# Layer 1 of a two-layer mixer and PEER kernel: the second table's products in two rounded parts

## The chip, the cores and the metric

The kernel runs on 1 core of a Trainium2 chip. The time is the device time of one execution in microseconds (us). The engines are called TensorE (PE; its weight loads are shown apart as PEld), VectorE (DVE), ScalarE (ACT), GpSimd (POOL) and SyncE (SP, which issues most transfers). The trace is of one profiled execution.

## What is computed

A backbone of two layers works on 256 latent tokens and 256 context tokens of width 1024. Each layer has a token mixer and then a feed-forward network of 16384 single-neuron experts (PEER). Only the latter matters here. For every token it chooses 16 experts for each of 8 heads, by two short lists of keys, and adds up the chosen rows of a second table, `v_tab`, each weighted by a softmax and by the gelu of the token's product with the row of a first table, `u_tab`:

```python
def peer_ffn(x, w_q, keys, u_tab, v_tab):
    def chunk(t):
        q = (t @ w_q).astype(jnp.float32).reshape(PEER_CHUNK, PEER_HEADS, 2, PEER_DK // 2)
        s = jnp.einsum("thpc,hpnc->thpn", q, kf)
        sv, si = lax.top_k(s, PEER_TOPK)
        ...
        best, pos = lax.top_k(cand, PEER_TOPK)
        eidx = jnp.take_along_axis(cidx, pos, axis=-1)
        g = jax.nn.softmax(best, axis=-1)
        act = jax.nn.gelu(jnp.einsum("thkd,td->thk", jnp.take(u_tab, eidx, axis=0), t).astype(jnp.float32))
        w = (g * act).astype(t.dtype)
        return jnp.einsum("thk,thkd->td", w, jnp.take(v_tab, eidx, axis=0))
```

The output is the latent stream after the second layer and a final norm.

## The kernel before

The program is a list of items for each layer: the mixer's, then the network's (`peer`). `Builder.run` goes through the list, and each item issues its instructions on all engines in the order of the code; nothing reorders them later, so the order of the items sets the order on every engine.

The network is computed densely for most tokens. Stage *up* (`up`, 128 items): for each block of 128 experts the first table's block times the tokens, with gelu, into the large buffer `A` (experts x blocks x tokens). Beside it DVE chooses the experts (`topk`, `weights`). Stage *experts* (`experts`, one item for four tokens): from the lists, one-hot matrices `oi` and `oj` are made, their product `psG` holds each token's softmax weights at its experts, and `A` is multiplied by it (L1366). Stage *down* (`down`, 126 items and one of two blocks): for each block of 128 experts, eight products of a 128x128 block of the second table with a row of `A`, summed over all blocks in four banks of PSUM called `acc`. `end` adds the sum to the stream and, in layer 1, applies the final norm. In layer 1 only 160 latent tokens go this way (N = 160; in layer 0 it is 256). The rest of the tokens, in layer 1 96, go the sparse way: their experts' rows are fetched one by one by GpSimd's indirect transfers (L1219) and added up by PE in `psC` with weights `wl` (`far_up`, `far_down`). Its steps are issued between the items by `far_go`, 18 of them in layer 1's *down*. What they fetch goes into the buffers `own` and `hs`, which the change leaves as they are. The last step copies `psC` into `ct` on ACT and turns it by eight transposes.

A product on PE comes in two forms. Unrounded: one matmul of 32-bit operands (L1502, layer 1's *down*; L1321, *up*). Rounded: both operands are given as a high part, rounded to the type fp32r, and a low part, the rest, rounded as well; `mm3` adds three matmuls of them, high by high, high by low and low by high (L200, L201, L202). The low by low product is left out. The mixers and layer 0's *down* use it. The parts are made by `cut` (for a half of a table's row block, 512 columns: a copy on ACT, L174, and a subtraction on DVE or GpSimd, L176 or L178; `lo_by` says on which, in *down* always DVE) and by `halves` (for `A`: L205, L206, called by `w_halves` for two blocks at once). `run` makes the cuts up to CUT = 5 halves ahead of the item that needs them.

The raw rows of the tables come by SP's transfers, 512 KB each. In layer 1 they go through a ring of eight buffers, five lent from the cuts' pool (`fetched`) and three of the pool `raw`; a ring piece is not cut, and its buffer is free again when its item is done. `self.lent` says that the cuts' own pool is lent away. Layer 1's network further has buffers of its own: `xe`, `h` (normed input), `qT` (queries), `rt` (routing: the lists' scratch), `keys`, `hs`, `own`, `wh` and `cand`. `h`, `qT`, `rt` and `keys` are last read before or during the *experts* stage's start; `wh` holds `oj` in that stage and then `ct`.

Of the kernel before, what the change touches and what calls it, by code (L numbers as in the profile page):

```python
# [69 lines left out]
class Builder:  # L70
# [21 lines left out]
    def run(self, items):  # L92
# [4 lines left out]
        cuts = [(p, h) for p in loads for h in range(p.cuts())]  # L97
        self.raws = self.rings = n_cut = used = n_ring = 0

        def load():  # L100
            nonlocal n_ring
            while rings and rings[0].ring == self.ring_for and self.rings < len(self.ring):
                p = rings.pop(0)
                p.raw = self.ring[n_ring % len(self.ring)]
                n_ring += 1
                self.rings += 1
                self.nc.sync.dma_start(out=p.raw[:, :p.width], in_=p.ap)
            while loads and self.raws < self.RAW and n_ring >= 16:
                p = loads.pop(0)
                p.at = n  # L110
                p.raw = self.wp.tile([128, 1024], F, tag="raw", name="raw", bufs=self.RAW)
                self.raws += 1
                self.nc.sync.dma_start(out=p.raw[:, :p.width], in_=p.ap)

        n = 0
        for n, it in enumerate(items):
            if n:
                load()
            now = used + sum(p.cuts() for p in it.pieces)
            while cuts and not self.lent and n_cut < used + self.CUT and cuts[0][0].raw is not None:  # L120
                if n_cut >= now and (n < max(cuts[0][0].at + self.AGE, self.FIRST) or not it.ahead):
                    break
                self.cut(*cuts.pop(0))
                n_cut += 1
                load()
            self.new = []
            it.fn(*it.pieces)
            used += sum(p.cuts() for p in it.pieces)
            self.raws -= sum(p.keep and p.ring is None for p in it.pieces)
            self.rings -= sum(p.ring is not None for p in it.pieces)  # L130
            self.tick()
# [27 lines left out]
    turn, lo_by, ring_for = 0, "vp", None  # L159
    lent = False  # L160
# [6 lines left out]
    def cut(self, p, h):  # L167
        nc = self.nc
        a, b = h * 512, min(h * 512 + 512, p.width)
        both = self.wp.tile([128, 2, 512], R, tag="cut", name="whl", bufs=self.CUT)  # L170
# [9 lines left out]
        if b == p.width and not p.keep:  # L180
            self.raws -= 1
# [825 lines left out]
    def peer(self, l, seg, far):  # L1007
# [27 lines left out]
        def begin():  # L1035
# [15 lines left out]
            else:  # L1051
                xs, h32, qT = (mp.tile([128, 8, 256], F, name=n) for n in ("xe", "h", "qT"))
                rt, keys = (mp.tile([128, 1024], F, name=n) for n in ("rt", "keys"))
# [302 lines left out]
        def experts(t4):  # L1356

            def fn():
# [15 lines left out]
                if t4 == N // 4 - 1:  # L1374
                    self.flush()
                    self.lo_by = self.LO_DOWN
            return Item(fn)


        def far_down():  # L1380
# [16 lines left out]
            for s, (tt, m) in enumerate(steps):  # L1397
# [22 lines left out]
                if m == nf - 1:  # L1420
                    while two and hold["i"] < 28:
                        yield False
                    ct = flat(A[:, 16:20]) if two else mp.tile([128, 2, 1024], F, tag="wh", name="ct")[:, 0]
# [51 lines left out]
        def down(i, n=1):  # L1475

            def fn(*ps):
                nonlocal wh
                hold["i"] = i
                if i == 0:  # L1480
# [3 lines left out]
                    if two:  # L1484
                        wh = mp.tile([128, 2, 4, 256], R, tag="wh", name="wh")
                        w_halves(0)
                if two:
                    if i % 2 == 0 and i < 126:
                        w_halves(i + 2)
# [6 lines left out]
                for d in range(8):  # L1496
                    for j, p in enumerate(ps):
                        acc, first, last = hold["acc"][d // 2][:, d % 2, :N], i == 0 and d % 2 == 0, i + j == 127
                        if two:
                            self.mm3(acc, p.block(d), wt[i + j], first, last, skip=True)  # L1500
                        else:
                            nc.tensor.matmul(acc, p.raw[:, d * 128:d * 128 + 128], A[:, i + j], start=first, stop=last,  # L1502
                                             skip_group_check=True)
# [5 lines left out]
            return Item(fn, *[Piece(t["peer_v"][l, j * 128:j * 128 + 128], 1024, split=two, ring=ring) for j in range(i, i + n)],  # L1509
# [160 lines left out]
```

## Time and profile before

| | us |
|---|---|
| median of 3 runs | 3388.54 (3386.39 to 3388.63) |
| profiled execution | 3395.13 |
| its span, first to last instruction | 3393.4 |
| in the span: layer 1's *experts* stage | 2984 to 3062 |
| layer 1's *down* | 3062 to 3379 |
| `end`, last part | 3379 to 3393 |

The profile is a page with the busy time of each engine, slices of the span and groups of instructions, and views of the trace that answer narrower questions. PE and PEld count instructions as the hardware records them: an unrounded matmul leaves two records, a rounded one leaves one, and each record has a weight load beside it. A matmul's duration reaches from its start to the modelled end of its pipeline, so records overlap, and the pace is read from start to start. "PEclk" is the granted clock of PE as a share of 2.4 GHz.

### The profile page before, as it was taken

The numbers are of one execution on the slowest core, as the hardware profiler recorded it, in microseconds if no ns is written. First come the engines' busy times: TensorE is split into PE (matmuls) and PEld (weight loads), VectorE is DVE, ScalarE is ACT, GpSimd is POOL, SyncE is SP. The second block draws the span as 40 slices with busy tenths as digits, with TensorE's granted clock in tenths as the row PEclk, the third lists the DMA queues.
The fourth block names the chain that finished last, engine by engine and source line by source line (L and its number), as shares of the span: only waits on it lengthen the run. The fifth ranks groups of instructions, "written<-read, shape, count | busy, mean of one in ns | idle before, by whom it ended". The sixth has DMA issues, their size and how long they took to land. (4 is left out here: it accounts for less than half of the span.)

```text
span 3393.4 us, 50776 instructions
## 1 busy us (share of the span) xinstructions
PE 3111.5 (92%) x19130; PEld 2514.0 (74%) x19130; DVE 1893.5 (56%) x4591; ACT 1076.3 (32%) x2268; POOL 1250.6 (37%) x1178
## 2 busy tenths in 40 slices
PE   7999999997799999588999998988998999989998
PEld 4667776785688788346777787667878899868897
DVE  6557444444799997866444455566444767660001
ACT  4554344331101101254333344554554110160000
POOL 2422223320254445674445512334453044372220
PEclk9999999998999999699999998999999999989999
DMA  7421221234699999976999966542235699968995
GB/s 273 156 98 57 68 60 60 87 118 149 228 400 387 375 378 407 333 255 229 343 373 393 392 242 214 168 134 87 95 100 172 213 387 408 402 209 312 353 354 184
DMA packets 245013, 819.03 MB, mean 241 GB/s; under 512 B 31776, under 2 KB 50464, under 8 KB 244512
## 3 DMA queue, kind: packets, MB, share of 16 engines
q1 hardware_dynamic: 137824, 441.40, 36.9%
q0 software_dynamic: 101376, 369.14, 29.1%
q10 hardware_dynamic: 5568, 5.24, 0.5%
q8 instruction: 151, 2.47, 0.3%
q14 instruction: 94, 0.77, 0.1%
HBM read 809.37 MB, written 6.29 MB: 240 GB/s over the span
## 5 line engine op out<-in xcount | busy, mean ns | idle before, releaser
L178 POOL TENSOR_TENSOR whl<-raw,whl 128x512 fp32r<-128x512 f32 x249 | 326.3, 1325 | 820.0 <-ACT whl L174 735.2
L176 DVE TENSOR_TENSOR whl<-raw,whl 128x512 fp32r<-128x512 f32 x359 | 277.6, 781 | 387.2 <-ACT whl L174 316.4
L1321 PE MATMUL psA<-hb,raw 128*128 128x256 f32 x2048 | 458.9, 383 | 14.6 <-DMA raw<-peer_u 12.7
L174 ACT ACTIVATE whl<-raw 128x512 fp32r<-128x512 f32 x608 | 362.0, 626 | 318.6 <-PE acc L202 249.3
L1321 PEld LDWEIGHTS psA<-hb,raw 128*128 128x128 f32 x2048 | 385.6, 191 | 80.9 <-issue 11.0
L200 PE MATMUL psA<-hhi,whl 128*128 128x512 f32 (+1 forms) x1032 | 375.6, 364 | 10.5 <-DVE bones L459 6.6
L201 PE MATMUL psA<-hlo,whl 128*128 128x512 f32 (+1 forms) x1032 | 365.3, 354 | 0.3 <-POOL hlo L506 0.3
L202 PE MATMUL psA<-hhi,whl 128*128 128x512 f32 (+1 forms) x1032 | 364.0, 353 | 0.9 <-DVE whl L176 0.9
L1219 POOL DMA_INDIRECT fetched<-u_rows,ft x184 | 184.0, 1000 | 322.9 <-PE psN L1214 136.6
L200 PE MATMUL acc<-wh,whl 128*128 128x256 f32 x1024 | 294.8, 288 | 1.4 <-ACT wh L205 1.4
L201 PE MATMUL acc<-wh,whl 128*128 128x256 f32 x1024 | 289.6, 283 | 0.8 <-issue 0.4
L202 PE MATMUL acc<-wh,whl 128*128 128x256 f32 x1024 | 289.4, 283 | 0.0
L1323 ACT ACTIVATE A<-psA 128x512 f32<-128x512 f32 (+1 forms) x128 | 66.2, 517 | 691.4 <-PE psA L1321 591.9
L200 PEld LDWEIGHTS psA<-hhi,whl 128*128 128x128 f32 x1032 | 198.7, 193 | 61.5 <-issue 26.5
L1250 DVE SCALAR_TENSOR_TENSOR fetched<-fetched,hT 128x1024 f32<-128x1024 f32 x184 | 221.3, 1209 | 22.1 <-DMA fetched<-u_rows,ft 15.5
L200 PEld LDWEIGHTS acc<-wh,whl 128*128 128x128 f32 x1024 | 195.9, 191 | 40.3 <-issue 23.5
L202 PEld LDWEIGHTS psA<-hhi,whl 128*128 128x128 f32 x1032 | 198.2, 192 | 28.0 <-DVE whl L176 1.9
L201 PEld LDWEIGHTS psA<-hlo,whl 128*128 128x128 f32 x1032 | 197.9, 192 | 25.0 <-POOL hlo L506 0.6
L201 PEld LDWEIGHTS acc<-wh,whl 128*128 128x128 f32 x1024 | 196.1, 192 | 0.5 <-DVE wh L206 0.5
L202 PEld LDWEIGHTS acc<-wh,whl 128*128 128x128 f32 x1024 | 196.1, 192 | 0.5 <-issue 0.5
L1219 POOL DMA_INDIRECT hb<-peer_v,ft x136 | 141.3, 1039 | 146.6 <-PE psC L1413 113.7
L1219 POOL DMA_INDIRECT own<-u_rows,ft x96 | 104.0, 1083 | 243.4 <-DVE own L1250 99.8
(372 smaller groups left out, 6043.9 us busy)
## 6 DMA issues: line engine op xcount, KB each, us to landing
raw<-peer_u SPq DMA_DIRECT2D x176, 512.0 KB
raw<-peer_v SPq DMA_DIRECT2D x176, 512.0 KB
raw<-w_in SPq DMA_DIRECT2D x126, 512.0 KB
ring<-w_mod SPq DMA_DIRECT2D x88, 512.0 KB
fetched<-peer_u SPq DMA_DIRECT2D x80, 512.0 KB
fetched<-peer_v SPq DMA_DIRECT2D x80, 512.0 KB
raw<-w_branch SPq DMA_DIRECT2D x32, 512.0 KB
raw<-w_out SPq DMA_DIRECT2D x16, 512.0 KB
```

The lines of the kernel that those rows point to most:

```text
L174: nc.scalar.activation(hx, x, AF.Copy)
L176: nc.vector.tensor_sub(lx, x, hx.bitcast(F))
L178: nc.gpsimd.tensor_sub(lx, x, hx.bitcast(F))
L200: mm(ps, wh, xh, start=start, stop=False, skip_group_check=skip)
L201: mm(ps, wh, xl, start=False, stop=False, skip_group_check=skip)
L202: mm(ps, wl, xh, start=False, stop=stop, skip_group_check=skip)
L1219: nc.gpsimd.indirect_dma_start(out=buf, out_offset=None, in_=rows, in_offset=bass.IndirectOffsetOnAxis(ap=idx.bitcast(I32), axis=0))
L1250: nc.vector.scalar_tensor_tensor(b, b, 1.0, h, op0=OP.mult, op1=OP.mult, accum_out=f[:, 3, k:k + 1])
L1321: nc.tensor.matmul(ps[:, :N], p.raw[:, k * 128:k * 128 + 128], h32[:, k, off:], start=k == 0, stop=k == 7)
L1323: nc.scalar.activation(A[:, i - 1:i + 1, :], hold["ps"][:, :, :N], AF.Gelu_apprx_tanh)
```

## The change

In layer 1's *down* the products are made as in layer 0, by `mm3` from two rounded parts. The ring's pieces of the second table are now split: `run` lists their cuts too (`pieces` in place of `loads`), notes when they were loaded, and gives a ring buffer back when its piece has been cut. `cut` takes its output from `cut_to`, where that is set, in place of the pool `cut`, which in layer 1 is lent to the ring. `cut_to` is set in the last `experts` item: six buffers of 128 x 2 x 512, two each in the place of `h`, `qT` and `rt`, for which `rt` and `keys` become two halves of one buffer; `lent` becomes false there, so that the cutting can begin with the first `down` item. The row of `A` is split by `w_halves` into `wh`, and `ct` moves from `wh` to `cand`.

```diff
@@ -94,13 +94,14 @@
         pieces = [p for it in items for p in it.pieces]
         loads = [p for p in pieces if p.ring is None]
         rings = [p for p in pieces if p.ring is not None]
-        cuts = [(p, h) for p in loads for h in range(p.cuts())]
+        cuts = [(p, h) for p in pieces for h in range(p.cuts())]
         self.raws = self.rings = n_cut = used = n_ring = 0
 
         def load():
             nonlocal n_ring
             while rings and rings[0].ring == self.ring_for and self.rings < len(self.ring):
                 p = rings.pop(0)
+                p.at = n
                 p.raw = self.ring[n_ring % len(self.ring)]
                 n_ring += 1
                 self.rings += 1
@@ -127,7 +128,7 @@
             it.fn(*it.pieces)
             used += sum(p.cuts() for p in it.pieces)
             self.raws -= sum(p.keep and p.ring is None for p in it.pieces)
-            self.rings -= sum(p.ring is not None for p in it.pieces)
+            self.rings -= sum(p.keep and p.ring is not None for p in it.pieces)
             self.tick()
 
 
@@ -157,6 +158,7 @@
             self.new = []
 
     turn, lo_by, ring_for = 0, "vp", None
+    cut_to = None
     lent = False
 
     def lo(self, l, i):
@@ -167,7 +169,10 @@
     def cut(self, p, h):
         nc = self.nc
         a, b = h * 512, min(h * 512 + 512, p.width)
-        both = self.wp.tile([128, 2, 512], R, tag="cut", name="whl", bufs=self.CUT)
+        if self.cut_to:
+            both = self.cut_to[self.turn % len(self.cut_to)]
+        else:
+            both = self.wp.tile([128, 2, 512], R, tag="cut", name="whl", bufs=self.CUT)
         hi, lo = both[:, 0], both[:, 1]
         p.parts.append((hi, lo))
         x, hx, lx = p.raw[:, a:b], hi[:, :b - a], lo[:, :b - a]
@@ -178,7 +183,10 @@
             nc.gpsimd.tensor_sub(lx, x, hx.bitcast(F))
         self.turn += 1
         if b == p.width and not p.keep:
-            self.raws -= 1
+            if p.ring is None:
+                self.raws -= 1
+            else:
+                self.rings -= 1
 
 
     def open(self, name, banks=True):
@@ -1049,8 +1057,9 @@
                 h32 = hb[:, 0]
                 own = [flat(hb[:, a, r:r + 4]) for a in range(2) for r in (0, 4)]
             else:
-                xs, h32, qT = (mp.tile([128, 8, 256], F, name=n) for n in ("xe", "h", "qT"))
-                rt, keys = (mp.tile([128, 1024], F, name=n) for n in ("rt", "keys"))
+                xs, h32, qT = (mp.tile([128, 8, 256], F, tag=n, name=n) for n in ("xe", "h", "qT"))
+                both = mp.tile([128, 2, 1024], F, tag="rt", name="rt")
+                rt, keys = both[:, 0], both[:, 1]
                 fq, fh = qT, h32
                 hs = mp.tile([128, 2, 1024], F, name="hs")
                 own = [mp.tile([128, 1024], F, name=f"own{i}") for i in range(6)]
@@ -1371,9 +1380,13 @@
                     if "far" not in hold:
                         hold["far"], hold["done"] = far_steps(), 0
                     far_go(EARLY + 1 if last else min(hold["done"] + 1, (EARLY + 1) * (t4 + 1) // (N // 4 - 4)))
-                if t4 == N // 4 - 1:
+                if last:
                     self.flush()
                     self.lo_by = self.LO_DOWN
+                    if not two:
+                        w = [mp.tile([128, 2, 2, 512], R, tag=tag, name="whl") for tag in ("h", "qT", "rt")]
+                        self.cut_to = [x[:, i] for x in w for i in range(2)]
+                        self.lent = False
             return Item(fn)
 
 
@@ -1420,7 +1433,7 @@
                 if m == nf - 1:
                     while two and hold["i"] < 28:
                         yield False
-                    ct = flat(A[:, 16:20]) if two else mp.tile([128, 2, 1024], F, tag="wh", name="ct")[:, 0]
+                    ct = flat(A[:, 16:20]) if two else mp.tile([128, 1024], F, tag="cand", name="ct", bufs=1)
                     for h in range(2):
                         nc.scalar.activation(ct[:, h * 512:h * 512 + 512], c[h], AF.Copy)
                     yield True
@@ -1481,12 +1494,11 @@
                     hold.pop("oj")
                     hold.pop("oi")
                     hold["acc"] = [psT([128, 2, 256], "acc") for _ in range(4)]
-                    if two:
-                        wh = mp.tile([128, 2, 4, 256], R, tag="wh", name="wh")
-                        w_halves(0)
+                    wh = mp.tile([128, 2, 4, N], R, tag="wh", name="wh")
+                    w_halves(0)
+                if i % 2 == 0 and i < 126:
+                    w_halves(i + 2)
                 if two:
-                    if i % 2 == 0 and i < 126:
-                        w_halves(i + 2)
                     if i == 28:
                         hold["xf"] = A[:, 20:28]
                         nc.sync.dma_start(out=hold["xf"], in_=self.xs[far])
@@ -1496,17 +1508,13 @@
                 for d in range(8):
                     for j, p in enumerate(ps):
                         acc, first, last = hold["acc"][d // 2][:, d % 2, :N], i == 0 and d % 2 == 0, i + j == 127
-                        if two:
-                            self.mm3(acc, p.block(d), wt[i + j], first, last, skip=True)
-                        else:
-                            nc.tensor.matmul(acc, p.raw[:, d * 128:d * 128 + 128], A[:, i + j], start=first, stop=last,
-                                             skip_group_check=True)
+                        self.mm3(acc, p.block(d), wt[i + j], first, last, skip=True)
                 for j in range(n):
                     wt.pop(i + j, None)
                 slow = 4 if two else 0
                 far_go(EARLY + (i + 1) // 4 if i < 4 * slow else
                        EARLY + slow + (FAR - EARLY - slow) * (i + 1 - 4 * slow) // (122 - 4 * slow))
-            return Item(fn, *[Piece(t["peer_v"][l, j * 128:j * 128 + 128], 1024, split=two, ring=ring) for j in range(i, i + n)],
+            return Item(fn, *[Piece(t["peer_v"][l, j * 128:j * 128 + 128], 1024, ring=ring) for j in range(i, i + n)],
                         ahead=i + n < 128)
 
         def end():
```

PE at the start of layer 1's *down* (`psC` is the sparse way's sum, `psG` the one-hot product, `acc` the dense sum). Before:

```order
L1413 MATMUL psC<-own_20866,wl 32x512
L1413 MATMUL psC<-hs,wl 32x512 x2
L1364 MATMUL psG<-oi,oj 128x128 x16
L1502 MATMUL acc<-A,fetched 128x160 x40
L1502 MATMUL acc<-A,raw 128x160 x24
L1502 MATMUL acc<-A,fetched 128x160 x32
```

And now:

```order
L1426 MATMUL psC<-own_20865,wl 32x512
L1426 MATMUL psC<-hs,wl 32x512 x2
L1373 MATMUL psG<-oi,oj 128x128 x16
L208 MATMUL acc<-wh,whl 128x160
L209 MATMUL acc<-wh,whl 128x160
L210 MATMUL acc<-wh,whl 128x160
```

Each product of 160 columns has become three, on the rounded parts `wh` and `whl`; what stands ahead and the places of `psC` between the blocks are as before.

DVE at the same place (`oi` and `oj` are the one-hot matrices, `wl` the sparse way's weights, `whl` a cut half, `wh` the split row of `A`). Before:

```order
L1366 TENSOR_TENSOR A<-A,psG 128x128x4
L1351 TENSOR_SCALAR oi<-iota,sel 128x128
L1352 TENSOR_TENSOR oj<-iota,sel 128x512
L1366 TENSOR_TENSOR A<-A,psG 128x128x4 x4
L1401 TENSOR_TENSOR wl<-ft,zero_20881 128x128 x18
L1432 SCALAR_TENSOR_TENSOR xe<-psX,mod_86,xe 128x96 x8
```

And now:

```order
L1375 TENSOR_TENSOR A<-A,psG 128x128x4
L1360 TENSOR_SCALAR oi<-iota,sel 128x128
L1361 TENSOR_TENSOR oj<-iota,sel 128x512
L1375 TENSOR_TENSOR A<-A,psG 128x128x4 x4
L181 TENSOR_TENSOR whl<-fetched,whl 128x512 x5
L214 TENSOR_TENSOR wh<-A,wh 128x320 x2
L181 TENSOR_TENSOR whl<-fetched,whl 128x512 x4
L214 TENSOR_TENSOR wh<-A,wh 128x320
```

Behind the last multiplications into `A`, where the 18 `wl` stood alone, five subtractions of cut halves now come first, then the first two pairs of `A`'s parts, and so on through the stage with the `wl` between them.

## Rows read from the trace of the kernel before

**Rows 1.** The page: span, busy us, share and instructions of the engines.

```profile
span 3393.4 us, 50776 instructions
PE 3111.5 (92%) x19130; PEld 2514.0 (74%) x19130; DVE 1893.5 (56%) x4591; ACT 1076.3 (32%) x2268; POOL 1250.6 (37%) x1178
```

**Rows 2.** Busy time by stretch: busy us and instructions, granted clock, DMA share, GB/s.

```profile
core 0: us, PE busy (x) PEld busy (x) DVE busy (x) ACT busy (x) POOL busy (x), PEclk, DMA share, GB/s
3062.00:3379.00 317.00, 316.26 (x2344) 287.07 (x2344) 10.48 (x38) 3.44 (x8) 64.27 (x67) 1.00 0.86 312
```

**Rows 3.** The chain that ended last: start us, us, engine, tile, line, instructions.

```profile
3062.23 26.35 PE acc L1502 x192
3088.58 1.85 PE psC L1413 x16
3090.43 13.24 PE acc L1502 x96
```

**Rows 4.** Groups from 3062 to 3379 us: busy us, mean ns, idle before, releaser.

```profile
L1502 PE MATMUL acc<-A,fetched 128*128 128x160 f32 x1280 | 179.5, 300 | 0.8 <-DVE A L1366 0.8
L1502 PE MATMUL acc<-A,raw 128*128 128x160 f32 x768 | 108.2, 300 | 0.0
L1413 PE MATMUL psC<-own,wl 128*32 128x512 f32 x216 | 34.5, 598 | 0.0
L1413 PE MATMUL psC<-hs,wl 128*32 128x512 f32 x72 | 17.2, 598 | 0.0
```

**Rows 5.** Instructions in order of time, PE, within layer 1's down.

```profile
3092.64 6.68 PE L1502 MATMUL acc<-A,raw 128*128 128x160 f32 x48
```

**Rows 6.** The same, PE in layer 0's down: rounded products, 256 columns.

```profile
2002.14 0.28 PE L200 MATMUL acc<-wh,whl 128*128 128x256 f32 x1
2002.26 0.28 PE L201 MATMUL acc<-wh,whl 128*128 128x256 f32 x1
```

**Rows 7.** The same, PE in layer 0's mixer: rounded products, 512 columns.

```profile
689.89 0.39 PE L200 MATMUL psA<-ohi,whl 128*128 128x512 f32 x1
...
692.15 0.39 PE L201 MATMUL psA<-hlo,whl 128*128 128x512 f32 x1
```

**Rows 8.** The same, weight loads in layer 0's down after a pause.

```profile
1614.51 0.19 PEld L200 LDWEIGHTS acc<-wh,whl 128*128 128x128 f32 x1 [0.84 <-ACT wh L205]
1614.61 0.19 PEld L201 LDWEIGHTS acc<-wh,whl 128*128 128x128 f32 x1
1614.73 0.19 PEld L202 LDWEIGHTS acc<-wh,whl 128*128 128x128 f32 x1
```

**Rows 9.** The same, weight loads of unrounded products with 96 columns.

```profile
429.80 1.86 PEld L212 LDWEIGHTS psT<-ones,sq 128*128 128x128 f32 x16 [1.61 <-ACT sq L816]
```

**Rows 10.** Groups from 1574 to 2048 us, layer 0's down.

```profile
L200 PEld LDWEIGHTS acc<-wh,whl 128*128 128x128 f32 x940 | 179.8, 191 | 38.6 <-issue 23.5 <-ACT wh L205 14.2 <-ACT whl L174 0.8
L176 DVE TENSOR_TENSOR whl<-raw,whl 128x512 fp32r<-128x512 f32 x233 | 160.0, 692 | 252.2 <-ACT whl L174 188.8 <-issue 60.0
L174 ACT ACTIVATE whl<-raw 128x512 fp32r<-128x512 f32 x234 | 146.2, 630 | 283.5 <-PE acc L202 243.4 <-DMA raw<-peer_v 19.0 <-issue 14.9
L206 DVE TENSOR_TENSOR wh<-A,wh 128x512 fp32r<-128x512 f32 x59 | 40.4, 685 | 0.0
```

**Rows 11.** Instructions in order of time where layer 1's down begins.

```profile
3061.49 0.69 DVE L1366 TENSOR_TENSOR A<-A,psG 128x512 f32<-128x512 f32 x1 [0.21 <-issue]
...
3062.23 11.13 PE L1502 MATMUL acc<-A,fetched 128*128 128x160 f32 x80 [0.78 <-DVE A L1366]
```

**Rows 12.** The same, PE where layer 0's down begins.

```profile
1573.20 0.38 PE L200 MATMUL acc<-wh,whl 128*128 128x256 f32 x1 [1.44 <-ACT wh L205]
...
1573.93 0.38 PE L201 MATMUL acc<-wh,whl 128*128 128x256 f32 x1 [0.34 <-DVE wh L206]
```

**Rows 13.** Busy time by stretch, columns as in rows 2.

```profile
2750.00:2800.00 50.00, 50.00 (x370) 49.42 (x369) 39.90 (x112) 4.81 (x11) 21.89 (x21) 1.00 1.02 408
```

**Rows 14.** Transfers from 3062 to 3379 us.

```profile
DMA packets 27129, 99.01 MB, mean 312 GB/s; under 512 B 3020, under 2 KB 3020, under 8 KB 27107
```

## The prediction

> **What bounds the kernel now.** I read the page first, for the shares of the engines [rows 1]: TensorE (PE) is busy for 92% of the span and, apart from its own weight loads, no other engine for more than 56%. That is a mean over very different stages, so the next view is the busy time by stretch [rows 2]. The change touches one stretch, the second table's products of layer 1, from 3062 us to 3379 us. There PE is busy for 316.26 of 317.00 us at a granted clock of 1.00, which is the upper of its two levels, 2.4 GHz. VectorE (DVE) works for 10.48 us of it, ScalarE (ACT) for 3.44 us, and the DMA moves 312 GB/s. The chain of waits says the same in another way [rows 3]: from 3062.23 us its links are two kinds of PE work in turn, 13.24 us for 96 records of the products `acc` and 1.85 us for the 16 records of `psC`, and so on to the stage's end. Nothing ends late there but PE, so this stage is worth exactly what its matmuls cost, and a change of their number or pace goes into the span in full. The groups of that stretch give the counts [rows 4]: 1280 + 768 = 2048 records of `acc` for 128 blocks of experts x 8 = 1024 products, two records for each unrounded product.
>
> **What the change removes.** It removes the 1024 unrounded products. In a stretch without interruption 48 records take 6.68 us, each 0.299 us long [rows 4, 5], so one starts every (6.68 - 0.30) / 47 = 0.1358 us, and 2048 of them cost 278.1 us. The rest of the stage stays: (216 + 72) / 16 = 18 steps of `psC` at 1.85 us, 33.3 us, and some 5 us of changes between the two kinds.
>
> **What it adds on PE.** Each product becomes three rounded ones of one record each (layer 0's rows show L200, L201 and L202 taking turns), so 3072 records, and each has its own load of 128 columns of weights. What one such record costs with 160 columns is the whole question, and the trace has no rounded product with fewer than 256 columns. It can be bounded from both sides:
>
> - With 256 columns a rounded record starts every 0.120 us [rows 6]; with 512 columns every 0.226 us: ten steps in 2.26 us from 689.89 to 692.15 [rows 7]. The slope is 0.107 us for 256 columns, with about 0.013 us on top. Carried on to 160 columns, that gives 0.067 + 0.013 = 0.080 us, if columns alone set the pace.
> - The weights must be loaded as well. In layer 0's rounded stream, just after a pause, when two loads may follow each other freely, they still start 0.10 us apart, and from then on 0.12 us [rows 8]. And where a product has so few columns that its streaming cannot hide the load, the load sets the pace: 16 unrounded records with 96 columns (2 x 96 = 192 columns streamed, which by the slope above would be done in 0.080 us) have loads that take 1.86 us from first start to last end, at 0.19 us each, so one every (1.86 - 0.19) / 15 = 0.111 us [rows 9].
>
> So I take max(0.080, 0.111), rounded to 0.112 us: a product with 160 rounded columns waits for its weights. It is the row nearest in kind, a stream whose columns take less than its load. 3072 x 0.112 = 344.1 us, which is 66.0 us more than the 278.1 us that go. The ends: at the 0.105 us that the closest pair of loads allows, 322.6 us, +44.5; at 0.120 us, the pace that layer 0's rounded stream really holds, 368.6 us, +90.5.
>
> The Trainium skill states a price for the load in "TensorE: Matmul & The Clock Gate", section "LDWEIGHTS (loading the stationary operand)": columns divided by 1.2 GHz, so 107 ns for 128. That rule speaks against this change, and the trace agrees with it (0.111 us by the 96-column stream). By it alone the sum would be 3072 x 0.107 = 328.7 us, an estimate, +50.6 us.
>
> **What it adds on ACT and DVE.** For each block two halves of the raw table are rounded (ACT) and subtracted (DVE), and for every second block a pair of the weights' columns. From layer 0's same stage: 0.630 us and 0.692 us a half, and on DVE 0.685 us a pair with 512 elements [rows 10]; layer 1's pair has 320, so that is an upper bound, and I take it for ACT too. For each block of 128 experts, ACT: 2 x 0.63 + 0.34 = 1.60 us. DVE: 2 x 0.69 + 0.34 = 1.72 us. PE needs 24 x 0.112 = 2.69 us. Both have over a third to spare, and both stand nearly idle there now [rows 2]. The rows of the order show the rounding up to five halves ahead, so the work hides, except once: at the stage's start. Now DVE's last multiplication into `A` starts at 3061.49, and PE begins its products at 3062.23 [rows 11]. After the change DVE has five subtractions and then the first pair's behind that multiplication, because cutting may only begin after the last `experts` item. The first rounded product starts as before, but the second needs the low part of the weights: 5 x 0.69 = 3.45 us later at most, with DVE starting its next instruction about 0.1 us before the last one's end, so about 3.4 us of PE idle. In layer 0, where the halves are cut earlier, that gap is 0.73 us, from 1573.20 to 1573.93 [rows 12].
>
> **What else moves.** The raw rows of the table stay in the same eight buffers, free after the cut instead of after the product, so a transfer can only start earlier. The stage moves 99.01 MB [rows 14]; in a longer stage that is 99 / 0.386 = 256 GB/s, and 408 GB/s were reached elsewhere [rows 13], so no transfer comes to bind. `ct` takes the place of `cand`, whose last reader is a stage back: nothing. `rt` and `keys` become two halves of one buffer: DVE's, GpSimd's and PE's order ahead of the stage is the same, and PE's waits there keep their places, so nothing. The new halves lie in `h`, `qT`, `rt` and `keys`, whose last readers are done before the experts' stage: no wait. GpSimd's fetches for `psC` keep their places between the same steps and just come further apart.
>
> **The sum.** +66.0 + 3.4 = +69.4 us. The profiled execution took 3395.13 us, of which the trace's span is 3393.4 us; it would become 3464.5 us. The median of the three runs is 3388.54 us, 6.6 us below it, and I forecast against the median: 3388.5 + 69.4 = 3458 us, 2.0% slower.
>
> **The rivals.** *Columns set the pace* (the other side of no change): if the load of the next weights hides fully behind 160 columns, a record costs 0.080 us, the products 245.8 us, and the sum is -32.3 + 3.4 = -28.9, so 3360 us. For it: the slope of the 256- and 512-column streams [rows 6, 7]. Against it: the loads are never closer than 0.10 us where nothing holds them, and set a pace of 0.111 us where the columns are few [rows 8, 9]. It decides as soon as a load takes under 0.090 us: 278.1 - 3.4 = 274.7 us over 3072. The DMA would allow it, 99 MB in 287 us being 345 GB/s. I give it 8%. The Trainium skill's page "TensorE: Matmul & The Clock Gate" has a rule that goes the same way and further, in section "Back-to-back issue gap": columns / 2.4 + 2.5 ns, so 69 ns here, 212 us for all, an estimate of some 3326 us. The trace does not agree: by that rule 256 columns would take 109 ns, and the rounded stream takes 120 [rows 6].
>
> *A rounded record with few columns costs as much as an unrounded one.* The unrounded record streams its columns twice (0.1358 us for 160). If the rounded one did so below 256 columns, 3072 x 0.1358 = 417.2 us, +142.5, so 3531 us; if it took the four passes of a whole unrounded product, 0.27 us each, some 3940 us. For it only that no row excludes it; against it that 256 and 512 columns lie on one line through a small rest. 8% together.
>
> *The cuts come late*: PE waits for ACT's low and high parts as in layer 0, where it lost 14.2 us on `wh` [rows 10]. There a full DMA and three raw buffers made the cuts late; here there are eight and the DMA has room. It would give 3458 + 14 = 3472 us. 12%, inside the range. That the change does not do what it says is excluded by its order, which shows three products in place of each one.
>
> **How the numbers follow.** Forecast 3458 us with 70%, late cuts 12%, columns 8%, dear records 8%, anything else 2%. The range must hold the first two with the bounds of the load: from +44.5 + 2 (3435 us) to +90.5 + 3.4 and some late cuts (3492 us); the other cases are the two tenths left out. A measurement of this kernel tells about 0.2% from no change. Faster 8%, within 0.2% 2%, slower 90%.
>
> **What would show it.** In the changed kernel's stretch from 3062 us: records of `acc` starting 0.112 us apart (0.080: the columns' rival; 0.136 or 0.27: the dear one; 0.120: the upper bound), loads just as far apart, PE over 98% busy, one PE pause of about 3.4 us at the start that DVE's `wh` ends, and the stage's end near 3448 us. A stage with PE idle on `wh` or `whl` again and again would mean late cuts. Wrong at the root would be a stage before 3062 us that moved.

## The result and the profile after

The changed kernel takes 3488.13 us (median of 4 runs, 3486.47 to 3489.82) against 3388.59 us (median of 4 as well): 1.0276 times as long, 95% interval 1.0259 to 1.0294, so +99.5 us. The forecast was 3458 us; the time lies in the upper part of the range of 3435 to 3492 us.

The page of the changed kernel, with the busy time of each engine and the granted clock in 40 slices:

```profile
span 3487.7 us, 53885 instructions
PE 3211.8 (92%) x20154; PEld 2612.2 (75%) x20154; DVE 2095.1 (60%) x4911; ACT 1258.6 (36%) x2588; POOL 1252.1 (36%) x1178
...
PEclk9999999999999998899999999999999999969999
```

PE has 1024 records more, 3072 for 2048 as forecast, and is as busy as in [rows 1]. New is the 6 in the row of the clock, in the slice from 3052 to 3139 us, where layer 1's *down* begins. The stretches of that stage, with the same columns as [rows 2]:

```profile
core 0: us, PE busy (x) PEld busy (x) DVE busy (x) ACT busy (x) POOL busy (x), PEclk, DMA share, GB/s
3060.00:3063.00 3.00, 0.35 (x2) 0.20 (x2) 3.00 (x7) 0.86 (x2) 2.15 (x3) 0.71 0.93 262
3063.00:3124.50 61.50, 61.50 (x291) 61.35 (x295) 19.53 (x31) 16.27 (x28) 0.00 (x0) 0.50 0.43 141
3127.10:3143.40 16.30, 16.30 (x152) 16.21 (x152) 8.70 (x14) 7.57 (x13) 3.79 (x4) 1.00 0.86 295
3060.00:3473.20 413.20, 410.55 (x3368) 382.18 (x3368) 211.44 (x356) 182.15 (x322) 65.97 (x67) 0.92 0.71 240
```

The stage lasts 413.2 us where it lasted 316.3: +96.9 us. The spans of the two profiled executions, 3487.7 and 3393.4 us, differ by 94.3 us; in the second the stage began 2.2 us earlier. PE works through all of it but 2.7 us, as in [rows 2], so late cuts are not the reason. But in its first 61.5 us the clock reads 0.50, the lower of its two levels, 1.2 GHz, with PE busy for every bit of it. The chain of waits shows where that ends (start us, us, engine, tile, line, instructions):

```profile
3124.51 2.64 PE psC L1426 x16
...
3143.39 1.85 PE psC L1426 x16
```

The first `psC` step of the stage still takes 2.64 us, all later ones the 1.85 us of [rows 3]. From behind it on the clock reads 1.00. The loads of weights on either side, in order of time:

```profile
3100.06 0.33 PEld L209 LDWEIGHTS acc<-wh,whl 128*128 128x128 f32 x1
3100.28 0.33 PEld L210 LDWEIGHTS acc<-wh,whl 128*128 128x128 f32 x1
...
3127.41 0.19 PEld L208 LDWEIGHTS acc<-wh,whl 128*128 128x128 f32 x1
3127.52 0.19 PEld L209 LDWEIGHTS acc<-wh,whl 128*128 128x128 f32 x1
```

At the upper level one load starts every 0.11 us: the pace that [rows 9] gave, and the forecast's term. At the lower level it is every 0.21 us. And this is the stage's start:

```profile
3059.40 3.14 DVE L181 TENSOR_TENSOR whl<-fetched,whl 128x512 fp32r<-128x512 f32 x5
3060.04 0.34 PE L208 MATMUL acc<-wh,whl 128*128 128x160 f32 x1 [1.28 <-ACT wh L213]
3062.46 0.88 DVE L214 TENSOR_TENSOR wh<-A,wh 128x320 fp32r<-128x320 f32 x2
3062.99 0.50 PE L209 MATMUL acc<-wh,whl 128*128 128x160 f32 x1 [2.61 <-DVE wh L214]
```

PE waits 1.28 us for ACT and then 2.61 us for DVE's `wh`, behind five subtractions, as forecast (about 3.4 us were). What the forecast did not have is what follows: the clock falls there and stays down for 12 blocks of products, until `psC`.

So the working theory after the result: +66 us for the loads (3072 records at 0.112 us for 2048 at 0.1358), some 3 us of waiting (1.28 and 2.61 us for the 0.78 of [rows 11]), and 288 records at 0.213 us (61.5 us over 288) in place of 0.112, which is 29 us. That adds up to 98 us for the 96.9. The rivals are that the start is slow for another reason (cuts, transfers), that the pause alone and not the kind of stream behind it costs the clock, and, for the loads, that columns set the pace after all.

### The profile page after: what moved, and what is told of

Read it like the earlier page. It is cut to its first block, busy times and chain, and to the rows that moved or that the text cites. A ratio compares the mean times of both kernels' runs of the same rounds, so it can differ in the third digit from the quotient of the medians.

```text
span 3487.7 us, 53885 instructions
## 1 busy us (share of the span) xinstructions
PE 3211.8 (92%) x20154; PEld 2612.2 (75%) x20154; DVE 2095.1 (60%) x4911; ACT 1258.6 (36%) x2588; POOL 1252.1 (36%) x1178
## 3 DMA queue, kind: packets, MB, share of 16 engines
q8 instruction: 159, 2.61, 0.3%
## 5 line engine op out<-in xcount | busy, mean ns | idle before, releaser
L181 DVE TENSOR_TENSOR whl<-raw,whl 128x512 fp32r<-128x512 f32 x455 | 342.9, 761 | 447.4 <-ACT whl L179 374.7
L208 PE MATMUL acc<-wh,whl 128*128 128x256 f32 (+1 forms) x2048 | 592.4, 289 | 2.7 <-ACT wh L213 2.7
L209 PE MATMUL acc<-wh,whl 128*128 128x256 f32 (+1 forms) x2048 | 585.9, 286 | 2.8 <-DVE wh L214 2.6
L210 PE MATMUL acc<-wh,whl 128*128 128x256 f32 (+1 forms) x2048 | 585.5, 286 | 0.0
L179 ACT ACTIVATE whl<-raw 128x512 fp32r<-128x512 f32 x704 | 422.7, 627 | 386.8 <-PE acc L210 239.5
L208 PEld LDWEIGHTS acc<-wh,whl 128*128 128x128 f32 x2048 | 406.8, 199 | 58.5 <-issue 26.8
L209 PEld LDWEIGHTS acc<-wh,whl 128*128 128x128 f32 x2048 | 407.0, 199 | 3.2 <-DVE wh L214 3.2
L210 PEld LDWEIGHTS acc<-wh,whl 128*128 128x128 f32 x2048 | 406.9, 199 | 0.0
```

What stands on the lines that cost most here:

```text
L179: nc.scalar.activation(hx, x, AF.Copy)
L181: nc.vector.tensor_sub(lx, x, hx.bitcast(F))
L208: mm(ps, wh, xh, start=start, stop=False, skip_group_check=skip)
L209: mm(ps, wh, xl, start=False, stop=False, skip_group_check=skip)
L210: mm(ps, wl, xh, start=False, stop=stop, skip_group_check=skip)
```

## The experiments

**The pause shortened.** The changed kernel with the first pair of `wh` split ahead of the cuts:

```diff
@@ experts(t4), last item
...
                     if not two:
+                        hold.pop("oj")
+                        hold.pop("oi")
+                        wh = mp.tile([128, 2, 4, N], R, tag="wh", name="wh")
+                        w_halves(0)
                         w = [mp.tile([128, 2, 2, 512], R, tag=tag, name="whl") for tag in ("h", "qT", "rt")]
...
```

> The changed kernel, except that layer 1's first pair of A's parts (wh) is split in the last experts item, ahead of the five cuts, so that DVE makes the low part first and PE has no pause of some 2.6 us before its second product. The products and their number stay. Theory (a record costs 0.112 us at the upper clock; the 0.213 us of the first 12 blocks is the lower clock, to which PE fell in that pause and which only the first psC step ended): the clock stays at 1.00, some 288 records lose 0.1 us each and the pause goes, -30 to -33 us against the changed kernel, about 3456 us. Rival (the first blocks are slow for another reason, such as the cuts or the transfers at the stage's start): only the pause goes, about 3485 us.

Measured: 3478.42 us, 1.0283 times the kernel before on that chip (1.0266 to 1.0301). The number that the theory gave was missed by 22 us; the rival's was 7 us off. The interval overlaps that of the changed kernel's 1.0276, so no gain is shown. PE at the stage's start in the timeline (start us, us, engine, line, instructions, wait and what ended it):

```profile
3041.97 0.34 PE L208 MATMUL acc<-wh,whl 128*128 128x160 f32 x1 [1.80 <-ACT whl L179]
3042.70 0.49 PE L210 MATMUL acc<-wh,whl 128*128 128x160 f32 x1 [0.27 <-DVE whl L181]
```

The two stretches behind it, with the columns of [rows 2]:

```profile
3044.00:3106.00 62.00, 62.00 (x294) 60.36 (x297) 21.73 (x35) 18.13 (x32) 0.06 (x1) 0.50 0.43 140
3109.00:3124.00 15.00, 15.00 (x137) 14.84 (x140) 8.80 (x14) 7.80 (x14) 2.83 (x3) 1.00 0.86 287
```

The 2.61 us became 0.27, but a wait of 1.80 us is left, which ACT's first cut into `whl` now ends. The clock falls all the same and stays at 0.50 until the first `psC`. So this pause was not needed for the fall. That leaves two readings: the gap that remains is enough, or the rounded stream loses the clock by itself. The filled gap, below, tells them apart.

**The first `psC` step earlier.**

```diff
-                far_go(EARLY + (i + 1) // 4 if i < 4 * slow else
+                far_go(EARLY + (i + 1) // 4 if i < 4 * slow else (0 if two or i == 0 else 2) +
```

> The changed kernel, except that the steps of the sparse way (psC) are issued about ten blocks earlier: the first one behind the second block of the products in place of the twelfth. All work stays, the pause too. Theory (the lower clock lasts until a psC step lifts it): the slow stretch shrinks from 12 blocks to 2, 240 records gain 0.1 us, -24 us against the changed kernel, about 3464 us. Rival (a slow start that ends by itself after some 60 us): no change, about 3488 us.

Measured: 3460.86 us, 1.0229 (1.0212 to 1.0246), 3 us from the theory's number. The first `psC` step of the stage in the chain of waits:

```profile
3068.57 2.58 PE psC L1426 x16
```

The stretches ahead of the first of them and behind it:

```profile
3057.00:3069.00 12.00, 10.75 (x51) 10.31 (x55) 4.48 (x9) 2.28 (x5) 0.94 (x1) 0.50 0.86 311
3071.00:3200.00 129.00, 129.00 (x1144) 118.27 (x1141) 69.83 (x113) 61.27 (x106) 31.15 (x32) 1.00 0.86 297
```

The slow stretch ends with the first `psC` step, wherever that stands: 12 us in place of 61. A start that is slow for its cuts or transfers would not have moved with it.

**The pause without the rounded products.** The kernel before, with five additional subtractions ahead of the last multiplication into `A`:

```diff
+                def mul():
+                    if last and not two:
+                        for _ in range(5):
+                            nc.vector.tensor_sub(h32[:, 0:2], h32[:, 2:4], h32[:, 4:6])
+                    nc.vector.tensor_mul(a, a, ps)
+                self.later(mul)
```

> The kernel before, with five additional subtractions of 128x512 on DVE (on a buffer that nobody reads any more) ahead of the last multiplication into A, so that PE pauses about 3 us before its unrounded products. Theory A (the pause costs so much only because the stream behind it is one that waits for its loads; the unrounded stream gets its clock back by itself): +3 to +6 us against the kernel before, 3392 to 3395 us. Theory B (any stream stays at the lower clock until the first psC step, 192 records at twice 0.136 us): +3 +26, about 3418 us.

Measured: 3387.12 us, 1.0011 (0.9998 to 1.0025) times the kernel before on that chip, so some +4 us (-1 to +8), as theory A has it. PE's wait in the timeline:

```profile
3057.88 4.37 PE L1508 MATMUL acc<-A,fetched 128*128 128x160 f32 x15 [3.42 <-DVE A L1372]
```

The stretch around that wait and the one behind it:

```profile
3053.00:3063.00 10.00, 6.58 (x27) 6.28 (x27) 5.07 (x9) 0.00 (x0) 4.13 (x4) 0.51 0.79 275
3064.00:3100.00 36.00, 36.00 (x268) 34.39 (x267) 0.29 (x1) 0.00 (x0) 3.83 (x4) 1.00 0.74 254
```

The clock is down here too, 0.51 in the mean around the wait of 3.42 us, but the unrounded stream has it back some 5 us after it begins, with no `psC` step between. So a pause of this length costs next to nothing ahead of the unrounded products, where the changed kernel lost 29 us behind its own.

**More columns.** 224 (`NP`) in place of 160, the additional ones zeros:

```diff
...
+                    wh = mp.tile([128, 2, 4, 256], R, tag="wh", name="wh")
+                    if not two:
+                        for z in range(2):
+                            nc.vector.memset(wh[:, z, :, N:224].bitcast(F), 0.0)
...
-                        acc, first, last = hold["acc"][d // 2][:, d % 2, :N], i == 0 and d % 2 == 0, i + j == 127
+                        acc, first, last = hold["acc"][d // 2][:, d % 2, :NP], i == 0 and d % 2 == 0, i + j == 127
```

> The changed kernel with 224 columns in each rounded product of layer 1 in place of 160; the 64 additional ones are zeros and their sums are read by nobody. Everything else stays. Theory (the load of 128 columns of weights sets the pace, 0.112 us, and 224 columns would by the slope of 0.107 us per 256 and 0.013 us on top take 0.107 us): records stay at 0.112 us, 3486 to 3492 us if the clock behaves as in the changed kernel, 3456 to 3460 us if the fuller stream gets its clock back by itself. Rival (each column costs its 1/2.4 ns): 64 / 2.4 = 27 ns more for each of 3072 records, +82 us, about 3570 us.

Measured: 3453.75 us, 1.0217 (1.0195 to 1.0240). With 40% more columns the kernel is faster than the changed one. The stage's first stretches:

```profile
3053.00:3058.00 5.00, 4.76 (x21) 4.52 (x22) 2.40 (x6) 0.63 (x1) 0.03 (x1) 0.50 0.99 354
3058.50:3100.00 41.50, 41.50 (x371) 39.95 (x371) 23.73 (x37) 21.42 (x37) 3.78 (x4) 1.00 0.69 238
```

Two loads behind them, in order of time:

```profile
3100.03 0.19 PEld L209 LDWEIGHTS acc<-wh,whl 128*128 128x128 f32 x1
3100.14 0.19 PEld L210 LDWEIGHTS acc<-wh,whl 128*128 128x128 f32 x1
```

Loads still start 0.11 us apart, so 64 columns more cost nothing a record; the rival's +82 us did not come. And this stream has its clock back after some 5 us, ahead of any `psC` step, although the wait ahead of its first product, 4.19 us, is longer than either of the changed kernel's.

**Fewer columns.** 96 of the 160 from the second block on:

```diff
-                        self.mm3(acc, p.block(d), wt[i + j], first, last, skip=True)
+                        x = wt[i + j]
+                        if not two and i:
+                            acc, x = acc[:, :96], [v[:, :96] for v in x]
+                        self.mm3(acc, p.block(d), x, first, last, skip=True)
```

> The changed kernel, but from the second block on layer 1's rounded products take only 96 of the 160 columns: the sums of 64 tokens are left out, the rest of the work stays. Theory (the load of 128 columns of weights sets the pace): fewer columns save nothing, records stay 0.112 us apart at the upper clock and 0.213 at the lower, 3480 to 3490 us if the clock rises and stays as in the changed kernel, and more, not less, if with even fewer columns it does not stay up. Rival (columns set the pace, 0.04 + 0.013 = 0.053 us a record): 3072 x 0.06 us less, about 3300 us.

Measured: 3739.83 us, 1.1030 (1.1003 to 1.1057). With 40% of the columns left out the kernel takes 250 us more. The stage in one stretch:

```profile
3042.00:3726.00 684.00, 681.12 (x3368) 626.75 (x3368) 215.24 (x356) 184.16 (x323) 65.39 (x67) 0.54 0.44 145
```

Its loads at the lower and at the upper level, in order of time:

```profile
3100.00 0.33 PEld L208 LDWEIGHTS acc<-wh,whl 128*128 128x128 f32 x1
3100.22 0.33 PEld L209 LDWEIGHTS acc<-wh,whl 128*128 128x128 f32 x1
...
3180.33 0.19 PEld L209 LDWEIGHTS acc<-wh,whl 128*128 128x128 f32 x1
3180.44 0.19 PEld L210 LDWEIGHTS acc<-wh,whl 128*128 128x128 f32 x1
```

The two paces are those of 160 columns, 0.21 and 0.11 us, so the columns are no part of them. The difference is the clock, 0.54 in the mean over the stage: at 160 columns it stays up once `psC` has lifted it, at 96 it falls again and again. Nor does each `psC` step lift it here. The first two steps in the chain of waits:

```profile
3106.68 3.57 PE psC L1426 x16
3141.14 3.57 PE psC L1426 x16
```

The stretch over both, the rise near the third step, and what follows:

```profile
3104.00:3175.00 71.00, 71.00 (x332) 64.87 (x331) 20.66 (x33) 17.84 (x31) 7.55 (x8) 0.50 0.47 155
3180.30:3183.30 3.00, 3.00 (x30) 3.00 (x29) 0.96 (x2) 1.26 (x2) 2.29 (x3) 1.00 0.68 208
3184.00:3206.00 22.00, 22.00 (x105) 22.00 (x104) 7.42 (x12) 6.12 (x11) 0.54 (x1) 0.50 0.52 178
```

The expectation had "more, not less" for that case, but no number; the change in time is all clock.

**The operands changed over.** If loads are what costs, few loads and long streams must pay. Here A's parts are the weights, six records a block with 512 columns in place of 24 with 160; 32 tokens go unrounded, beside each other in the array; eight transposes turn the sums at the end. Its core:

```diff
+                        xh, xl = wt[i + j]
+                        for h, (hi, lo) in enumerate(p.parts):
+                            self.mm3(hold["acc"][h], (xh[:, :128], xl[:, :128]), (hi, lo), i + j == 0, i + j == 127, skip=True)
+                        pair.append((i + j, p.raw))
+                    if len(pair) == 2:
+                        for g in range(4):
+                            b, raw = pair[g // 2]
+                            nc.tensor.matmul(hold["acc"][2][32 * g:32 * g + 32, :], A[:, b, 128:N],
+                                             raw[:, g % 2 * 512:g % 2 * 512 + 512], start=b < 2, stop=b >= 126,
+                                             skip_group_check=True)
```

> The same sums with the operands changed over: the rounded parts of A (128 of the 160 tokens) are loaded as weights and the halves of the table's row block stream as 512 columns, six records for a block instead of 24. The other 32 tokens go unrounded, four matmuls of 32-column weights for two blocks beside each other in the array, as psC does. At the end eight transposes turn the sums; the cuts are as in the changed kernel, the first pair of wh is split early. Theory (few loads, long streams): 6 x 0.227 + 0.43 = 1.79 us a block, 229 us in place of the 278 of the kernel before, about 5 us more at the end, and full streams that hold the clock: some 42 us below the kernel before, 3343 us where that takes 3385. Rival (then the transfers bind: 99 MB at the 350 GB/s that the stage held before take 283 us): about 3357 us. If loads cost no more than columns, there would be nothing to win over the changed kernel's 0.112 us a record but the number of records.

Measured: 3371.27 us, 0.9942 times the kernel before (0.9927 to 0.9958): some 19 us faster than that, where the changed kernel is at 1.0276. It beats both, by less than forecast. PE over one pair of blocks and the start of the next:

```profile
3208.85 0.50 PE L208 MATMUL acc<-whl,wh 128*128 128x512 f32 x1
...
3211.27 0.40 PE L209 MATMUL acc<-whl,wh 128*128 128x512 f32 x1
3211.50 0.39 PE L210 MATMUL acc<-whl,wh 128*128 128x512 f32 x1
3211.82 1.06 PE L1528 MATMUL acc<-fetched,A 128*32 128x512 f32 x8
3212.82 0.50 PE L208 MATMUL acc<-whl,wh 128*128 128x512 f32 x1
3213.15 0.39 PE L209 MATMUL acc<-whl,wh 128*128 128x512 f32 x1
```

The stage but for its ends, in one stretch:

```profile
3062.00:3350.00 288.00, 287.06 (x1582) 157.41 (x1580) 195.53 (x339) 173.07 (x313) 70.23 (x64) 1.00 0.88 337
```

Records take the 0.23 us of [rows 7], and PE waits for nothing, so transfers do not bind. (The rival's 350 GB/s is misread: the stage before held 312 [rows 14]; here it is 337.) Missing from the forecast is the price of going from one kind of product to the other: the 32-column group takes 1.00 us to the next product's start, not 0.86, and the product ahead of it and the first behind it each keep PE 0.1 us longer (3211.50 to 3211.82 is 0.32 and 3212.82 to 3213.15 is 0.33, not 0.23). Two blocks so take 3.97 us, from 3208.85 to 3212.82, in place of 3.58, which over 64 pairs is 25 us.

**The operands changed over, unrounded.** The kernel before in the same order, core:

```diff
+                        for h in range(2):
+                            nc.tensor.matmul(hold["acc"][h], A[:, i + j, :128], p.raw[:, h * 512:h * 512 + 512],
+                                             start=i + j == 0, stop=i + j == 127, skip_group_check=True)
```

> The kernel before with its unrounded products of layer 1 changed over in the same way: A's 128 tokens as weights, 512 columns of the table streaming, nothing rounded, no cuts; the 32 other tokens as in e6_swapped. Theory (the unrounded form streams each column twice in each of two records, and its loads were hidden already): 4 x 0.429 + 0.43 = 2.15 us a block against 2.17, so -3 us and +5 us at the end: 3384 to 3392 us, no change, so that what e6_swapped gains comes from the rounded form once its loads are few. Rival (the gain lies in the changed-over order itself): as e6_swapped, some 3345 us.

Measured: 3406.77 us, 1.0046 (1.0028 to 1.0065): +16 us, slower than the "no change" expected and far from the rival's 3345. Two blocks:

```profile
3242.78 3.70 PE L1504 MATMUL acc<-fetched,A 128*128 128x512 f32 x8
3246.41 1.06 PE L1510 MATMUL acc<-fetched,A 128*32 128x512 f32 x8
3247.40 2.84 PE L1504 MATMUL acc<-fetched,A 128*128 128x512 f32 x6
```

From 3242.78 to 3247.40 two blocks take 4.62 us, 2.31 a block and not 2.15: the same price of the changes. The order alone wins nothing; it wins with the rounded form, whose loads then are few.

**The gap filled.** The first experiment's kernel with three matmuls in the gap that it left:

```diff
+                        fill = psH([128, 512], "fill")
+                        for _ in range(3):
+                            nc.tensor.matmul(fill, xs[:, 0, 0:128], flat(xs[:, 1:3]), start=True, stop=True)
```

> e1_no_pause with three additional unrounded matmuls of 512 columns (on the residual, into a free bank that nobody reads) between the last one-hot product and the first rounded one, 3 x 0.86 = 2.6 us of PE work that fills the gap of some 1.3 us which was left there. Theory (the lower clock comes from PE's gaps at the change of stage, which e1 shortened but did not close, and the rounded stream does not get the clock back by itself): the clock stays at 1.00 from the stage's start, the first 12 blocks take 0.112 us a record, some 30 us below the changed kernel on the same chip less about 2 us of filler: +66 to +70 us against the kernel before. Rival (the rounded stream with 160 columns loses the clock by itself at its start, whatever stands ahead of it): as e1_no_pause or 1 us above, +90 us or more.

> The changed kernel once more, on the same chip as e8_filled_gap, so that the two can be compared: +97 to +101 us against the kernel before, as measured, with the lower clock from the stage's start to the first psC step.

Measured on one chip: 3454.64 us with the gap filled, 1.0166 (1.0145 to 1.0187); 3485.47 us for the changed kernel once more, 1.0255 (1.0236 to 1.0274). So -31 us between the two. PE at the stage's start in the timeline:

```profile
3056.47 2.74 PE L1394 MATMUL fill<-xe 128*128 128x512 f32 x6
3058.65 0.64 PE L208 MATMUL acc<-wh,whl 128*128 128x160 f32 x1
```

The first `psC` step of the stage in the chain of waits:

```profile
3091.34 1.85 PE psC L1434 x16
```

The stretch ahead of that step, and the stage from its first product on:

```profile
3059.00:3090.00 31.00, 31.00 (x279) 30.95 (x278) 21.23 (x35) 17.93 (x33) 1.23 (x2) 1.00 0.79 273
3059.00:3439.00 380.00, 380.00 (x3368) 352.56 (x3367) 210.41 (x355) 183.42 (x324) 64.92 (x66) 1.00 0.76 260
```

The clock reads 1.00 from the first rounded product on, for over 30 us ahead of the first `psC` step. In the changed kernel once more, the stretch ahead of that step is again at the lower level:

```profile
3071.00:3132.00 61.00, 61.00 (x288) 60.85 (x288) 19.08 (x30) 16.27 (x28) 0.00 (x0) 0.50 0.40 138
```

So the stream with 160 columns holds the upper level when it begins at it, and behind the gaps did not come back to it by itself in the 61 us that it had. The stage with the gap filled lasts some 380 us: 64 us more than before, which is the loads' term. What remains of the changed kernel's +97 us is the clock and the waits. Against the kernel before on that chip it is +56 us by the ratio (49 to 64), below the 66 to 70 us of the forecast. The changed kernel once more misses its forecast of +97 to +101 us in the same way: it is +87 us by the ratio (80 to 93). On this chip the kernel before took 3396.26 us, 8 us more than in the first measurement, and the changed one did not; why is not known. The difference of 31 us between the two is what the forecast gave, and the stage itself shows the 64.

## Why the prediction was right, and where not

- *PE alone sets the stage, all of it goes into the span*: right. The stage grew by 96.9 us, the profiled span by 94.3, the median time by 99.5.
- *The load of 128 columns sets a pace of 0.112 us a record*: right in the pace, and the basis of the direction (how far the load is shown to be its cause stands below). 160, 224 and 96 columns all gave 0.11 us at the upper level. The rule of the Trainium skill in "TensorE: Matmul & The Clock Gate", section "LDWEIGHTS (loading the stationary operand)", columns over 1.2 GHz, so by estimate 107 ns for 128, is 4% below that and holds for the upper level alone: at the lower one a load started every 213 ns. The runs decide there.
- *Cuts on ACT and DVE are hidden*: right; in the changed kernel's stage, from its first product on, PE is idle for 2.7 us in all, nearly all of it in the pause.
- *A pause of about 3.4 us at the start, ended by DVE's `wh`*: right in kind and place, 2.61 us behind one of 1.28 us on ACT, where the kernel before had 0.78 us [rows 11].
- *The size*: the step that failed is the term "3072 x 0.112 = 344.1 us". It took the upper clock for all records, as in [rows 2], where the clock reads 1.00 all through; but that row is of an unrounded stream. 288 of the records ran at 0.213 us, 29 us more than the term has. The text said of the pause what it costs in waiting and nothing of what follows it. The range held the time because its upper end was made from 0.120 us a record and some late cuts, and neither came true: it held by luck, for the wrong reason. (The lower end's 0.105 us stands in no row; [rows 8] have pairs of loads 0.10 and 0.12 us apart. Nothing hangs on it.)
- *The rivals*: columns as the pace and dear records are both excluded by 224 and 96 columns; late cuts by the idle time. The Trainium skill's rule in "TensorE: Matmul & The Clock Gate", section "Back-to-back issue gap", columns / 2.4 + 2.5 ns, so by estimate 69 ns for 160 columns, agrees with no run here, where records start 0.11 us apart; that section itself says that the rule leaves out the load of weights.

A rival that the prediction does not have is a fixed price of 0.112 us for each record, whatever its load. No experiment changed the columns of the weights in rounded products. The trace of the kernel before bears on it in part, with two loads of unrounded products whose weights have 32 columns:

```profile
2708.20 0.14 PEld L1236 LDWEIGHTS hT<-ident,h 128*32 128x32 f32 x2 [0.18 <-issue]
```

Each of them is 0.11 us long and both are done in 0.14 us, so the second starts 0.03 us behind the first: a load of fewer columns costs less. That a rounded record with a shorter load would start earlier as well is likely by that, but not shown. That the columns that stream do not set the pace, between 96 and 224, is shown.

What made the clock fall at the start is not in every part shown. Filling the gaps kept it up, and shortening one of them did not. But the filler is also work of another kind, six records of 512 columns, and no run tells the closed gap from the work that closed it. A row of the kernel before could have warned: in the *experts* stage ahead, where PE works 60 of 78 us, its clock already reads 0.87 in the mean:

```profile
2984.00:3062.00 78.00, 60.06 (x419) 47.64 (x417) 58.96 (x120) 54.00 (x149) 68.35 (x67) 0.87 0.61 199
```

## What to carry to other kernels

Before a product is put in more passes, compare the time of its columns with the time of its weight load: below the load, columns were free here and each further record cost a full load, 0.112 us. Do not take the clock of a stretch over from another kind of stream: ask what the new one does after a gap, since the same 160 columns held the upper level when they began at it and stayed at the lower one for 61 us behind a gap. If it must begin behind one, long unrounded matmuls ahead of it or among its first blocks brought the clock back here, but with 96 columns not each time. Where a rounded operand has few columns, make it the weights and let the long one stream.

## What was not expected of the hardware

- PE busy without a gap for 61.5 us, by its records, at the lower clock level throughout (0.50), ended by one `psC` step of 16 records with 512 columns. With 96 columns the mean clock of 684 us of busy PE was 0.54, and the first two `psC` steps did not lift it; with 224 it rose by itself within some 5 us.
- The pace of the loads follows the clock: 0.112 us at the upper level, 0.213 at the lower.
- Going from 128-column products to groups of 32 columns and back costs PE some 0.1 us each way; with the group's own 1.00 us for 0.86 it took 25 us of the gain of the operands changed over.
